# A conditioned hybrid decoder layer: adaLN sums of three row tiles on VectorE, adaLN columns through HBM, HGRN2's output gates by column

## The chip, the cores and the metric

The kernel runs on one core of a Trainium2 chip. A core has TensorE for matrix products, VectorE and ScalarE for elementwise work, GpSimd as a slower helper, and SyncE (SP), whose queue issues nearly all of this kernel's DMAs. The metric is device time in microseconds of one execution. The kernel before took 730.64 us, the median of 3 runs (730.37 to 730.97).

## The reference, cut to what matters

The layer works on x of 512 tokens by 1024 columns, with a conditioning vector c of 1024.

```python
cs = silu(c)
mod = cs @ w_ada + b_ada                      # 6 x 1024
sh1, sc1, gt1, sh2, sc2, gt2 = split(mod, 6)
h = rmsnorm(x, norm1_g) * (1 + sc1) + sh1
z = h @ w_in                                  # 3352 columns: hq hf hi hg | q kc vc ks vs kw vw g
o_hg  = hgrn2(hq, hf, hi, hg)                 # 4 heads of 128; rmsnorm(o, norm_g) * silu(hg) at its end
o_nsa = nsa(...)                              # 8 heads of 64, rope on q and k, three branches
x = x + gt1 * (concat(o_hg, o_nsa) @ w_out)
h2 = rmsnorm(x, norm2_g) * (1 + sc2) + sh2
a, v = split(causal_dwconv(h2 @ w_up, conv_w, conv_b), 2)
x = x + gt2 * ((silu(a) * v) @ w_down)
```

Rope turns the first 16 columns of each 64-wide head by angles that depend on the token's position and eight fixed frequencies.

## The kernel before, in words

All dense products are done with operands split into a high and a low part in a rounded 32-bit format, three matmuls for one product (`mm3`: high by high, high by low, low by high; lines 132, 133 and 134 of the profile). `split` makes the parts: ScalarE copies the high part (line 128), VectorE subtracts it for the low part (line 129). The order of all instructions is written out by hand: every engine works through its own list in the order of the program, and generators are interleaved by `emit`.

**First projection (lines 567 to 606).** The 1024 columns of h are eight row tiles k of 128 (columns of h lie on partitions, tokens run along the free dimension). For each k, four accumulators `accq` (one for each 128 tokens) and two `accf` take 18 matmuls of 512 columns. Ahead of use, h of tile k+1 is made: `ada_row(k+1)` sums cs times w_ada's two 128-wide columns for shift and scale with eight matmuls of 32 stationary columns (line 384, into the tile that the warm-up used before, so the rows read `warm<-ada,cs`), ScalarE copies the 256 sums (line 388), and `ada_col` turns them into two columns with two matmuls against a selecting vector `sel` (line 395). `h_tile` then makes the factors on VectorE (lines 399, 400), applies them on ScalarE (line 417), copies the high part on ScalarE (line 418) and subtracts on VectorE (line 419). The row matmuls stand in front of tile k's 18 matmuls, the column after the first three.

The loads of this stage come in order on SP's queue: x, then for each k four pieces of w_ada (line 280, 1 MB in all), a piece of the q weights (line 299) and, for every second k, one of the forget-gate weights (line 302). In the step k = 0, after the loads of tile 3, `load_small` loads the rest of the constants (263 KB; masks and rope frequencies), the positions and the gains (lines 313 to 317). The first weights of the k and v projection follow (line 206). The rope tables (`all_tables`) are made in five steps, one after each `h_tile`: nothing, gate tables, first reduction of the angle, second reduction, sine and cosine with GpSimd's products.

**Attention beside dense work (about 120 to 304 us).** The generator `attn` does scores, exponents, transpositions (`F`, line 991) and values (`oT`, line 1019) in units. ScalarE copies the transposed probabilities out (line 998) into tiles of a pool of 32 buffers that also holds most long-lived tiles. Beside it run HGRN2's level products and the dense projections. `proj_tok` gives tokens on partitions with 256-wide matmuls (tile `pt`); `proj_T` gives columns on partitions with 512-wide ones (tile `pT`, written `pT<-hT,whi`). HGRN2's gates (`hg_gate_out`) come from `proj_tok`. Each of the two takes eight steps per pair of heads. Every few units attention calls the next step of `adas`: for the second sub-layer's shift and scale, `ada_cols` multiplies a quarter (256 columns) of w_ada by cs (line 1241), ScalarE copies the sums, and two matmuls against a column of ones (line 1272) make columns of them, which VectorE adds to the bias. `ada_rows` does likewise for gt1, spread over all partitions.

**Output projection (304 to 372 us).** For each 128 tokens i, `hg_mix` multiplies HGRN2's values, normalises on VectorE (line 1206) and multiplies by the gates (line 1209); `hg_flip` transposes (line 1217) and makes the high part on ScalarE and the low part on VectorE (lines 1220, 1221) with the norm's gain. `out_mm` multiplies by w_out, first attention's half, then HGRN2's. From 345 us on the second norm uses `a2` and `sh2` (lines 1412, 1414), and the up and down projections follow to the end.

Of the kernel before, what the change touches and what calls it, by code (L numbers as in the profile page):

```python
# [19 lines left out]
P = 128  # L20
# [30 lines left out]
PREP4 = ('', 'la1 na3 fa3', '', 'la2', '', 'la3', '', '')  # L51
LEVELS = (1, 2, 4, 8, 16, 32, 64)

C_IDENT = 0
C_LMASK = 128
# [3 lines left out]
C_INV = C_BLK + 4  # L59
C_ANY = C_INV + 8  # L60
# [28 lines left out]
def hybrid_layer_kernel(ctx: ExitStack, tc: tile.TileContext, d: dict, out: bass.AP, dbg=None):  # L89
# [8 lines left out]
    psum = ctx.enter_context(tc.tile_pool(name="psum", bufs=8, space=PSUM))  # L98
    ctx.enter_context(tc.manual_schedule())
# [132 lines left out]
    def piece(g=False):  # L232

        name, _, _ = loads[taken[0] - 1] if ahead_raw else loads[taken[0]]
        if not ahead_raw:
            raw = take(name)
            if name.startswith(("hq", "hf", "hvo")):
# [25 lines left out]
    sc.dma_start(cb[:, 0:P], d["consts"][:, 0:P])  # L263
# [48 lines left out]
    def load_small():  # L312
        sp.dma_start(cb[:, P:], d["consts"][:, P:])
# [63 lines left out]
    def ada_row(k):  # L377

        c0 = k % 2 * 256
        for j in range(KT):
            g = 32 * (j % 4)
            pe.matmul(rows[g:g + 32, c0:c0 + 256], cs32[:, j],
                      ada[k][j // 4][:, j % 4].rearrange("p e c -> p (e c)"),
                      start=(j < 4), stop=(j >= 4), skip_group_check=True)
        t = TMP([P, 256], tag="row")
        sc.copy(t, rows[:, c0:c0 + 256])
        return t

    def ada_col(k, t):

        adc = adcs[0][:, 2 * k:2 * k + 2]
        for e in range(2):
            pe.matmul(adc[:, e:e + 1], t[:, e * P:e * P + P], sel, start=True, stop=True)
        return adc
# [36 lines left out]
    def gate_tables():  # L433
        gp.tensor_copy(identb, ident)
        gp.tensor_copy(causb, cb[:, C_CAUS:C_CAUS + P])
# [17 lines left out]
    def all_tables():  # L453
        yield
# [4 lines left out]
        sc.copy(ctab, gains.unsqueeze(1).to_broadcast([P, NT, 4, HD]))  # L459
# [16 lines left out]
        for m in (2048.0, 1.0):  # L476
# [4 lines left out]
            yield  # L481
        ve.tensor_scalar(ang, ang, 3.1415925, -3.1415925, ALU.min, ALU.max)
        sc.activation(sn, ang, AF.Sin)
        sc.activation(co, ang, AF.Sin, scale=0.5)
        ve.tensor_tensor(co, co, co, ALU.mult)
# [67 lines left out]
    row = ada_row(0)  # L553
# [3 lines left out]
    adc = ada_col(0, row)  # L557
# [10 lines left out]
    for k in range(KT):  # L568
        h = hT[k]
        if k + 1 < KT:  # L570
# [9 lines left out]
            wn = first_weights(k + 1)  # L580
            wfn = first_gates(k + 1)
        if k == KT - 1:
            for _ in tables:
                pass
            piece()
        if k == 0:
            for e, f in ((0, 0), (0, 1), (1, 0)):
# [3 lines left out]
                if e + f == 0:  # L591
                    row = ada_row(1)
                elif f:
                    h_tile(1, ada_col(1, row))
                    next(tables, None)
        for i in range(NT if k else 0):
            sl = slice(i * P, (i + 1) * P)
            if k + 1 < KT and i == 1:
                h_tile(k + 1, ada_col(k + 1, row))
                next(tables, None)  # L600
# [4 lines left out]
        if k + 1 < KT:  # L605
            w, wfk = wn, wfn
# [565 lines left out]
    def hg_gate_out(pr):  # L1172
        def f(hb, a):
            if hb == 0:
                HGT[pr] = G([NT, 256], s="hgt")
# [10 lines left out]
    def hg_mix(i):  # L1186
# [21 lines left out]
        for pr in range(2):  # L1208
            ve.tensor_tensor(on[:, 2 * pr:2 * pr + 2], on[:, 2 * pr:2 * pr + 2],
                             HGT[pr][:, i].rearrange("p (h e) -> p h e", h=2), ALU.mult)  # L1210
        ons[i] = on

    def hg_flip(i):
# [5 lines left out]
        pv = ps.rearrange("p (h t) -> p h t", h=4)  # L1219
        sc.activation(m[:, 0], pv, AF.Copy, scale=hgg)  # L1220
        ve.scalar_tensor_tensor(m[:, 1], pv, hgg, f32(m[:, 0]), ALU.mult, ALU.subtract)
# [41 lines left out]
    def ada_cols(s, dst, bias, gain=None):  # L1263

        for q in range(4):
            sums = ada_quarter()
            rows = TMP([P, 512], tag="arow")
            sc.activation(rows[:, 0:256], sums, AF.Copy, scale=1.0 / 32)
            yield
            ps = PS()  # L1270
            for k in range(2):
                pe.matmul(ps[:, k:k + 1], rows[:, k * P:(k + 1) * P], ones[:, 0:1], start=True, stop=True)
            sl = slice(2 * q, 2 * q + 2)
            ve.tensor_tensor(dst[:, sl], ps[:, 0:2], bias[:, sl], ALU.add)
            if gain is not None:
                ve.tensor_tensor(dst[:, sl], dst[:, sl], gain[:, sl], ALU.mult)
            yield
# [66 lines left out]

    kv = proj_kv()
# [102 lines left out]
    out_mm(0, 0, KN)  # L1448
    hg_mix(1)
# [144 lines left out]
```

## Time and profile before

| what | value |
|---|---|
| median of 3 runs | 730.64 us |
| the profiled execution's own time | 730.55 us |
| its span, first to last instruction | 728.8 us |
| TensorE busy | 722.0 us (99%) |
| VectorE, ScalarE, GpSimd busy | 423.5, 329.5, 107.2 us |
| DMA moved | 90.22 MB, 124 GB/s on average |
| granted TensorE clock, mean | 0.999 |

Times are microseconds from the span's start. PE is TensorE's matmul queue, PEld its weight loads, DVE is VectorE, ACT ScalarE, POOL GpSimd, SPq SyncE's queue of DMA issues. A matmul's duration reaches past the start of the next, since matmuls are pipelined: what one costs is the distance between starts.

### The profile page before, as it was taken

Reading aid. Unit: us, or ns where it says so; the run is one execution under the profiler, and the core shown is the slowest. Engines: PE = TensorE matmul, PEld = TensorE weight load, DVE = VectorE, ACT = ScalarE, POOL = GpSimd, SP = SyncE. Lnnn points to the kernel's source line nnn. Section 1 sums busy time; section 2 is a strip of 40 time slices with the busy share of each in tenths; the row PEclk is TensorE's granted clock in tenths of the full one; section 3 lists DMA queues with packets and bytes.
Section 4 is the critical chain, followed back from the end, with each engine's and each line's share of the span. In section 5 each row is a group of like instructions: output and inputs, shape, how many; then the busy total and the mean of one; then the engine's idle time right before and its main releaser. Section 6 shows DMA issues by size and latency. Waiting matters only on the chain.

```text
span 728.8 us, 10806 instructions
## 1 busy us (share of the span) xinstructions
PE 722.0 (99%) x4275; PEld 595.0 (82%) x4275; DVE 423.5 (58%) x804; ACT 329.5 (45%) x632; POOL 107.2 (15%) x99
## 2 busy tenths in 40 slices
PE   8999999999999999999999999999999999999997
PEld 4678898787888888888898888888888888888886
DVE  5447587856867775567856666665555455224223
ACT  5555446655557565634563354344343443121220
POOL 1013020200000000010006536541101101000000
PEclk9999999999999999999999999999999999999999
DMA  9984171365233311724223534533442431325311
GB/s 287 289 261 130 33 232 58 126 185 164 92 130 117 116 59 59 270 77 121 59 58 116 174 98 133 167 84 96 116 113 62 116 115 61 114 86 174 98 47 58
DMA packets 109319, 90.22 MB, mean 124 GB/s; under 512 B 5555, under 2 KB 95187, under 8 KB 109269
## 3 DMA queue, kind: packets, MB, share of 16 engines
q1 hardware_dynamic: 109013, 89.43, 40.3%
q8 instruction: 34, 0.56, 0.3%
q10 hardware_dynamic: 256, 0.10, 0.1%
q14 instruction: 16, 0.13, 0.1%
HBM read 87.42 MB, written 2.10 MB: 123 GB/s over the span
## 4 chain that ended last, share of the span: by engine, by line
PE 92%; SPq 3%; DMA 2%; DVE 1%; issue 0%; ACT 0%; ACTq 0%
PE u L132 11%; PE u L133 11%; PE u L134 11%; PE dn L133 5%; PE dn L134 5%; PE dn L132 5%; PE oT L1019 3%; PE F L991 3%; PE pT L132 2%; PE pT L134 2%; PE pT L133 2%; PE oh L132 2%; PE oh L134 2%; PE oh L133 2%; PE S L939 2%; SPq L280 2%
## 5 line engine op out<-in xcount | busy, mean ns | idle before, releaser
L129 DVE TENSOR_TENSOR wlo<-raw,whi 128x1024 fp32r<-128x1024 f32 (+1 forms) x87 | 111.8, 1285 | 146.3 <-ACT whi L128 145.9
L132 PE MATMUL u<-h2h,whi 128*128 128x512 f32 (+1 forms) x360 | 136.7, 380 | 0.0
L133 PE MATMUL u<-h2l,whi 128*128 128x512 f32 (+1 forms) x360 | 136.7, 380 | 0.0
L134 PE MATMUL u<-h2h,wlo 128*128 128x512 f32 (+1 forms) x360 | 136.7, 380 | 0.0
L128 ACT CAST whi<-raw 128x1024 fp32r<-128x1024 f32 (+1 forms) x87 | 89.8, 1032 | 96.1 <-PE dn L134 80.0
L134 PEld LDWEIGHTS u<-h2h,wlo 128*128 128x128 f32 x360 | 67.7, 188 | 12.9
L132 PEld LDWEIGHTS u<-h2h,whi 128*128 128x128 f32 x360 | 67.7, 188 | 12.8
L133 PEld LDWEIGHTS u<-h2l,whi 128*128 128x128 f32 x360 | 67.7, 188 | 12.7
L133 PE MATMUL dn<-wlo,gT 128*128 128x512 f32 x160 | 62.3, 390 | 0.0
L134 PE MATMUL dn<-whi,gT 128*128 128x512 f32 x160 | 62.3, 389 | 0.0
L132 PE MATMUL dn<-whi,gT 128*128 128x512 f32 x160 | 62.2, 389 | 0.0
L356 POOL TENSOR_TENSOR hrs<-hrs,mhalf 128x4 f32<-128x4 f32 (+2 forms) x16 | 17.7, 1112 | 238.2 <-DVE hrs L355 238.2
L1500 POOL TENSOR_TENSOR y<-y,y 128x512 f32<-128x512 f32 x22 | 28.4, 1290 | 165.1 <-DVE y L1495 161.4
L128 ACT CAST gT<-y 128x512 fp32r<-128x512 f32 x20 | 12.4, 622 | 71.1 <-POOL y L1500 71.1
L960 ACT ACTIVATE pt<-S,mx 128x128 f32<-128x128 f32 (+3 forms) x64 | 33.8, 533 | 17.6 <-DVE mx L943 17.4
L129 DVE TENSOR_TENSOR gT<-y,gT 128x512 fp32r<-128x512 f32 x20 | 15.6, 782 | 42.8 <-ACT gT L128 42.8
L998 ACT COPY pT<-F 128x512 f32<-128x512 f32 (+2 forms) x52 | 26.2, 504 | 24.5 <-PE F L991 24.5
L1498 ACT ACTIVATE y<-y 128x512 f32<-128x512 f32 x22 | 13.9, 632 | 50.4 <-DVE y L1495 50.4
L943 DVE TENSOR_REDUCE mx<-S 128x1 f32<-128x384 f32 (+3 forms) x48 | 28.4, 597 | 14.2 <-PE S L941 14.1
L133 PEld LDWEIGHTS dn<-wlo,gT 128*128 128x128 f32 x160 | 30.0, 188 | 6.5 <-DVE wlo L129 0.2
L132 PEld LDWEIGHTS dn<-whi,gT 128*128 128x128 f32 x160 | 30.0, 188 | 6.3
L134 PEld LDWEIGHTS dn<-whi,gT 128*128 128x128 f32 x160 | 30.0, 188 | 6.1
(335 smaller groups left out, 1511.1 us busy)
## 6 DMA issues: line engine op xcount, KB each, us to landing
raw<-in_w_up SPq DMA_DIRECT2D x44, 512.0 KB, 4.0
aw<-in_w_ada SPq DMA_DIRECT2D x12, 1024.0 KB, 5.3
raw<-in_w_down SPq DMA_DIRECT2D x10, 1024.0 KB, 5.2
ada<-in_w_ada SPq DMA_DIRECT2D x32, 256.0 KB, 5.9
raw<-in_w_in SPq DMA_DIRECT2D x7, 1024.0 KB, 6.6
x<-in_x SPq DMA_DIRECT2D x8, 512.0 KB, 5.5
raw<-in_w_cmp SPq DMA_DIRECT2D x8, 512.0 KB, 4.9
raw<-in_w_out SPq DMA_DIRECT2D x4, 1024.0 KB, 5.0
```

The costliest lines, as they stand in the source:

```text
L128: sc.copy(hi, src)
L129: (eng or ve).tensor_tensor(lo, src, f32(hi), ALU.subtract)
L132: pe.matmul(o, ah, bh, start=start, stop=False, skip_group_check=True)
L133: pe.matmul(o, ah, bl, start=False, stop=False, skip_group_check=True)
L134: pe.matmul(o, al, bh, start=False, stop=stop, skip_group_check=True)
L356: gp.tensor_tensor(o, o, mhalf[:, 0:n], ALU.pow)
L943: ve.tensor_reduce(mx[:, 0:n], ps[:, 0:n * W].rearrange("p (b w) -> p b w", b=n), AX.X, ALU.max, negate=True)
L960: sc.activation(pt[:, sl], ps[:, sl], AF.Exp, bias=mx[:, e:e + 1], accum_out=su[:, h % 2, e:e + 1])
L991: pe.transpose(ps[:, j * P:(j + 1) * P], src[:, j * P:(j + 1) * P], ident)
L998: sc.copy(pT, ps[:, 0:n * P])
L1019: pe.matmul(oTs[i][r:r + 64, h // 2], VV[:, j, b, g], src[:, q * P:(q + 1) * P], start=(h == 0 and b == 0 and j == 0), stop=False, skip_gr ...
L1500: gp.tensor_tensor(ys[0], ys[0], y, ALU.mult)
```

## The change

It has five parts.

- The adaLN rows of tiles 4, 6 and 7 are no longer summed on TensorE. `ada_sum` does it on VectorE: eight instructions of 128x256 that multiply w_ada's piece by cs per partition and add up; the column is then made against a vector of ones. The steps are placed inside `h_tile` of tiles 3, 5 and 6, one tile earlier than the column's use: four, five and five of them before the subtraction for the low part of h, the rest behind it. The place of the column among the matmuls changes for tiles 4, 6 and 7, and the last tile's high part comes directly from the scaling.
- The small loads go before the loads of tile 3, the 263 KB of masks behind those of tile 7, and the frequencies of rope come with the first load of constants. The steps of the rope tables are cut differently and are made after tiles 1, 2, 4, 5 and 7.
- `ada_cols` no longer makes columns on TensorE. The four partial rows of each vector are stored to HBM, read back as 64 rows of 128 after attention, transposed once and added up on VectorE (`cols_sum`).
- HGRN2's gates are projected by column (`proj_T`). They are multiplied in after the transposition in `hg_flip`, together with the gain, and the split follows.
- The piece of the k and v weights for the end of the first projection is made before the last tables.

```diff
+ROWS = (2, 3, 5)
+COLS = (0, 0, 1, 1, 2, 1, 2, 2)
+SUMS = {3: (4, 4, 4), 5: (6, 5, 3), 6: (7, 5, 3)}
+QUICK = 7
...
+    def ada_sum(k):
+        t = TMP([P, 2, P], tag="rows")
+        arow[k] = t, ones[:, 0:1]
+        for j in range(KT):
+            w = ada[k][j // 4][:, j % 4]
+            if j:
+                ve.scalar_tensor_tensor(t, w, cs[:, j:j + 1], t, ALU.mult, ALU.add)
+            else:
+                ve.tensor_scalar(t, w, cs[:, 0:1], None, ALU.mult)
+            yield
...
     def h_tile(k, adc):
...
-        sc.activation(xk, xk, AF.Identity, bias=sh1[:, k:k + 1], scale=a1[:, k:k + 1])
-        sc.copy(h[:, 0], xk)
+        if k == QUICK:
+            sc.activation(h[:, 0], xk, AF.Identity, bias=sh1[:, k:k + 1], scale=a1[:, k:k + 1])
+            t = TMP([P, T], tag="ht")
+            ve.tensor_scalar(t, xk, a1[:, k:k + 1], sh1[:, k:k + 1], ALU.mult, ALU.add)
+            xk = t
+        else:
+            sc.activation(xk, xk, AF.Identity, bias=sh1[:, k:k + 1], scale=a1[:, k:k + 1])
+            sc.copy(h[:, 0], xk)
+        if k in SUMS:
+            sums = ada_sum(SUMS[k][0])
+            for _ in range(SUMS[k][1]):
+                next(sums)
         ve.tensor_tensor(h[:, 1], xk, f32(h[:, 0]), ALU.subtract)
         hT.append(h)
+        if k in SUMS:
+            for _ in range(SUMS[k][2]):
+                next(sums)
...
+                if k == 0:
+                    load_small()
                 load_ada()
                 load_qf()
-                if k == 0:
-                    load_small()
+                if k == 4:
+                    sp.dma_start(cb[:, C_LMASK:], d["consts"][:, C_LMASK:])
...
-            if k:
-                row = ada_row(k + 1)
+            if n in ROWS:
+                ada_row(n)
...
-            if k + 1 < KT and i == 1:
-                h_tile(k + 1, ada_col(k + 1, row))
-                next(tables, None)
+            if n < KT and i == COLS[n]:
+                h_tile(n, ada_col(n))
+                if k in (1, 3, 4, 6):
+                    next(tables, None)
...
     def hg_gate_out(pr):
-            ve.scalar_tensor_tensor(HGT[pr][:, 2 * hb:2 * hb + 2].rearrange("p i c -> p (i c)"), th, 1.0, a,
-                                    ALU.add, ALU.mult)
+            ve.scalar_tensor_tensor(HGT[pr][:, j], th, 1.0, a, ALU.add, ALU.mult)
...
-        for pr in range(2):
-            ve.tensor_tensor(on[:, 2 * pr:2 * pr + 2], on[:, 2 * pr:2 * pr + 2],
-                             HGT[pr][:, i].rearrange("p (h e) -> p h e", h=2), ALU.mult)
...
-        sc.activation(m[:, 0], pv, AF.Copy, scale=hgg)
-        ve.scalar_tensor_tensor(m[:, 1], pv, hgg, f32(m[:, 0]), ALU.mult, ALU.subtract)
+        t = TMP([P, 4, P], tag="og")
+        for pr in range(2):
+            ve.scalar_tensor_tensor(t[:, 2 * pr:2 * pr + 2], ps[:, pr * 256:pr * 256 + 256]
+                                    .rearrange("p (h t) -> p h t", h=2), hgg,
+                                    HGT[pr][:, :, i * P:(i + 1) * P], ALU.mult, ALU.mult)
+        split(m[:, 0], m[:, 1], t)
...
     def ada_cols(s, dst, bias, gain=None):
+        rows = G([D], s="arow")
         for q in range(4):
             sums = ada_quarter()
-            rows = TMP([P, 512], tag="arow")
-            sc.activation(rows[:, 0:256], sums, AF.Copy, scale=1.0 / 32)
+            sc.copy(rows[:, q * 256:q * 256 + 256], sums)
             yield
-            ps = PS()
-            for k in range(2):
-                pe.matmul(ps[:, k:k + 1], rows[:, k * P:(k + 1) * P], ones[:, 0:1], start=True, stop=True)
-            sl = slice(2 * q, 2 * q + 2)
-            ve.tensor_tensor(dst[:, sl], ps[:, 0:2], bias[:, sl], ALU.add)
+            if q == 3:
+                sp.dma_start(adr[4 * len(late_cols):4 * len(late_cols) + 4], rows[0:P:32])
+                late_cols.append((dst, bias, gain))
+            yield
+    adr = hbm.tile([8, D], F32, name="adr")
+    def cols_load():
+        r = TMP([64, P], tag="acol")
+        sp.dma_start(r, adr.rearrange("g (k p) -> (g k) p", p=P))
+        return r
+    def cols_sum(r):
+        ps = PS()
+        pe.transpose(ps[:, 0:64], r, ident[0:64, 0:64])
+        for n, (dst, bias, gain) in enumerate(late_cols):
+            ve.tensor_reduce(dst, ps[:, 32 * n:32 * n + 32].rearrange("p (g k) -> p k g", g=4), AX.X, ALU.add)
+            ve.tensor_tensor(dst, dst, bias, ALU.add)
...
-    dense = chain(hv0, hg_value_odd(), proj_tok(hg_gate_out(0)), proj_tok(hg_gate_out(1), False), late())
+    dense = chain(hv0, hg_value_odd(), proj_T(hg_gate_out(0)), proj_T(hg_gate_out(1), False), late())
...
     for _ in adas:
         pass
+    acol = cols_load()
...
     out_mm(0, 0, KN)
+    cols_sum(acol)
     hg_mix(1)
```

## Rows read from the trace of the kernel before

**Rows 1.** The page: busy us, share of the span, instructions of each engine.
```profile
PE 722.0 (99%) x4275; PEld 595.0 (82%) x4275; DVE 423.5 (58%) x804; ACT 329.5 (45%) x632; POOL 107.2 (15%) x99
```
**Rows 2.** Stretches: length, then busy time of PE, PEld, DVE, ACT, POOL.
```profile
146.00:304.00 158.00, 158.00 (x1432) 132.27 (x1431) 103.24 (x255) 94.79 (x228) 0.00 (x0) 1.00 0.41 132
```
**Rows 3.** Stretches, row tiles k=6 and k=7 of the first projection.
```profile
52.15:57.88 5.73, 5.73 (x40) 4.36 (x40) 2.21 (x6) 3.28 (x5) 0.00 (x0) 1.00 0.32 90
57.88:61.95 4.07, 4.07 (x19) 3.38 (x18) 2.55 (x5) 2.96 (x4) 1.59 (x1) 1.00 0.97 323
```
**Rows 4.** The chain that ended last, 30 to 47 us: start, length, what.
```profile
33.09 7.79 DMA ada<-in_w_ada
```
**Rows 5.** Timeline of TensorE, first projection: start, duration, what.
```profile
34.41 1.07 PE L384 MATMUL warm<-ada,cs 128*32 128x256 f32 x16
35.41 0.50 PE L132 MATMUL accq<-wq,hT 128*128 128x512 f32 x1
...
36.22 0.50 PE L395 MATMUL adc<-sel,row 128*128 128x1 f32 x4
...
47.92 0.40 PE L134 MATMUL accq<-wq,hT 128*128 128x512 f32 x1
...
53.73 0.40 PE L134 MATMUL accq<-wq,hT 128*128 128x512 f32 x1
```
**Rows 6.** VectorE groups by shape: count, busy us, mean ns, idle before.
```profile
L862 DVE SCALAR_TENSOR_TENSOR chs<-cth,cps 128x256 f32<-128x256 f32 x1 | 0.4, 421 | 0.6 <-ACT cth L860 0.6
```
**Rows 7.** Timeline of VectorE, first projection.
```profile
43.31 0.21 DVE L400 SCALAR_TENSOR_TENSOR a<-adc,bsc,vt 128x1 f32<-128x1 f32 x1
...
51.79 0.69 DVE L419 TENSOR_TENSOR hT<-xnT,hT 128x512 fp32r<-128x512 f32 x1 [1.54 <-ACT hT L418]
```
**Rows 8.** Timeline of SP's DMA issues, w_ada's tiles 5, 6 and 7.
```profile
31.46 3.51 SPq L280 DMA_DIRECT2D ada<-in_w_ada  x4
...
36.37 3.79 SPq L280 DMA_DIRECT2D ada<-in_w_ada  x4
...
42.05 3.00 SPq L280 DMA_DIRECT2D ada<-in_w_ada  x4
```
**Rows 9.** Stretches of 2 us; the last number is GB/s moved.
```profile
26.00:28.00 2.00, 2.00 (x10) 1.66 (x9) 0.53 (x3) 1.40 (x3) 0.00 (x0) 1.00 1.05 305
28.00:30.00 2.00, 2.00 (x21) 0.98 (x21) 1.25 (x6) 0.90 (x6) 0.00 (x0) 1.00 0.76 188
...
48.00:50.00 2.00, 2.00 (x12) 1.69 (x11) 1.60 (x3) 0.89 (x2) 2.00 (x4) 1.00 1.07 365
```
**Rows 10.** Timeline of TensorE, one quarter's columns and what follows.
```profile
254.97 0.50 PE L1272 MATMUL ps<-ones,arow 128*128 128x1 f32 x4
255.41 1.53 PE L1019 MATMUL oT<-pT,VV 128*64 128x128 f32 x24
```
**Rows 11.** Stretch, line 1272 alone: length, PE busy, PEld busy.
```profile
146.00:304.00 158.00, 4.13 (x32) 4.28 (x32) 1.00 0.41 132
```
**Rows 12.** Timeline of SP's issues, end of attention.
```profile
292.71 2.11 SPq L1446 DMA_DIRECT2D x<-in_x  x4
```
**Rows 13.** Timeline of TensorE: one step of each projection and its successor.
```profile
208.36 0.48 PE L132 MATMUL pT<-hT,whi 128*128 128x512 f32 x1
...
209.82 0.49 PE L991 MATMUL F<-cb,pt 128*128 128x128 f32 x3
...
250.94 0.36 PE L132 MATMUL pt<-whi,hT 128*128 128x256 f32 x1
...
252.45 0.49 PE L991 MATMUL F<-cb,pt 128*128 128x128 f32 x3
```
**Rows 14.** Timelines of VectorE and TensorE, HGRN2's last mixed tile.
```profile
330.52 0.75 DVE L1221 SCALAR_TENSOR_TENSOR mixH<-ps,hgg,mixH 128x512 fp32r<-128x512 f32 x1 [2.24 <-ACT mixH L1220]
...
335.01 0.39 PE L132 MATMUL oh<-woh,mixH 128*128 128x512 f32 x1
```
**Rows 15.** Stretch, line 998 alone: length, ScalarE busy and copies.
```profile
142.00:254.00 112.00, 14.97 (x31) 1.00 0.46 142
```

More of the change, by code (lines that the diff above doesn't have):

```diff
@@ L51 @@
 PREP4 = ('', 'la1 na3 fa3', '', 'la2', '', 'la3', '', '')
+ROWS = (2, 3, 5)
+COLS = (0, 0, 1, 1, 2, 1, 2, 2)
+SUMS = {3: (4, 4, 4), 5: (6, 5, 3), 6: (7, 5, 3)}
+QUICK = 7
 LEVELS = (1, 2, 4, 8, 16, 32, 64)
 C_IDENT = 0
-C_LMASK = 128
+C_INV = 128
+C_LMASK = 136
 C_CMASK = C_LMASK + sum(P // n for n in LEVELS)
@@ L58 @@
 C_BLK = C_CAUS + P
-C_INV = C_BLK + 4
-C_ANY = C_INV + 8
+C_ANY = C_BLK + 4
 C_COLS = C_ANY + NT
@@ L98, in hybrid_layer_kernel @@
     psum = ctx.enter_context(tc.tile_pool(name="psum", bufs=8, space=PSUM))
+    hbm = ctx.enter_context(tc.tile_pool(name="hbm", bufs=1, space=bass.MemoryType.DRAM))
     ctx.enter_context(tc.manual_schedule())
@@ L262, in hybrid_layer_kernel @@
     cb = cst.tile([P, C_COLS], F32, name="cb")
-    sc.dma_start(cb[:, 0:P], d["consts"][:, 0:P])
+    sc.dma_start(cb[:, 0:C_LMASK], d["consts"][:, 0:C_LMASK])
     ident = cb[:, C_IDENT:C_IDENT + P]
@@ L386, in ada_row, with ada_col @@
                       start=(j < 4), stop=(j >= 4), skip_group_check=True)
[L387 to L391, printed above, removed]
+        t = TMP([P, 2, P], tag="row")
+        sc.copy(t.rearrange("p e c -> p (e c)"), rows[:, c0:c0 + 256])
+        arow[k] = t, sel
+    def ada_sum(k):
[8 more added lines that the diff above has]
+            yield
+    arow = {}
+    def ada_col(k):
         adc = adcs[0][:, 2 * k:2 * k + 2]
+        t, one = arow.pop(k)
         for e in range(2):
-            pe.matmul(adc[:, e:e + 1], t[:, e * P:e * P + P], sel, start=True, stop=True)
+            pe.matmul(adc[:, e:e + 1], t[:, e], one, start=True, stop=True)
         return adc
@@ L458, in all_tables @@
         gp.tensor_scalar(gains[:, 0], gains[:, 0], HD ** -0.5, None, ALU.mult)
-        sc.copy(ctab, gains.unsqueeze(1).to_broadcast([P, NT, 4, HD]))
         posf = cst.tile([P, NT], F32, name="posf")
@@ L480, in all_tables @@
                 ve.scalar_tensor_tensor(ang, rnd, -pc * m, ang, ALU.mult, ALU.add)
-            yield
+            if m > 1.0:
+                yield
         ve.tensor_scalar(ang, ang, 3.1415925, -3.1415925, ALU.min, ALU.max)
+        sc.copy(ctab, gains.unsqueeze(1).to_broadcast([P, NT, 4, HD]))
+        yield
         sc.activation(sn, ang, AF.Sin)
         sc.activation(co, ang, AF.Sin, scale=0.5)
+        yield
         ve.tensor_tensor(co, co, co, ALU.mult)
@@ L552, in hybrid_layer_kernel @@
     x_scale(3)
-    row = ada_row(0)
+    ada_row(0)
     xn_out(2, 0, ve.tensor_copy, fl[2, 0])
@@ L556, in hybrid_layer_kernel @@
     xn_out(3, 0, ve.tensor_copy, fl[3, 0], (0,))
-    adc = ada_col(0, row)
+    adc = ada_col(0)
     fl[3, 1] = xn_flip(3, 1)
@@ L569, in hybrid_layer_kernel @@
         h = hT[k]
-        if k + 1 < KT:
+        n = k + 1
+        if n < KT:
             if k + 3 < KT:
+                if k == 0:
+                    load_small()
                 load_ada()
                 load_qf()
-                if k == 0:
-                    load_small()
+                if k == 4:
+                    sp.dma_start(cb[:, C_LMASK:], d["consts"][:, C_LMASK:])
             elif k + 3 == KT:
                 issue()
-            if k:
-                row = ada_row(k + 1)
-            wn = first_weights(k + 1)
-            wfn = first_gates(k + 1)
+            if n in ROWS:
+                ada_row(n)
+            wn = first_weights(n)
+            wfn = first_gates(n)
         if k == KT - 1:
+            piece()
             for _ in tables:
                 pass
-            piece()
         if k == 0:
@@ L591, in hybrid_layer_kernel @@
                 if e + f == 0:
-                    row = ada_row(1)
+                    ada_row(1)
                 elif f:
-                    h_tile(1, ada_col(1, row))
-                    next(tables, None)
+                    h_tile(1, ada_col(1))
+                    next(tables)
         for i in range(NT if k else 0):
             sl = slice(i * P, (i + 1) * P)
-            if k + 1 < KT and i == 1:
-                h_tile(k + 1, ada_col(k + 1, row))
-                next(tables, None)
+            if n < KT and i == COLS[n]:
+                h_tile(n, ada_col(n))
+                if k in (1, 3, 4, 6):
+                    next(tables, None)
             mm3(accq[i], h[:, 0, sl], h[:, 1, sl], w[:, 0], w[:, 1], False, k == KT - 1)
@@ L604, in hybrid_layer_kernel @@
             mm3(accf[j], wfk[:, 0, k % 2, sl], wfk[:, 1, k % 2, sl], h[:, 0], h[:, 1], k == 0, k == KT - 1)
-        if k + 1 < KT:
+        if n < KT:
             w, wfk = wn, wfn
@@ L1172, in hg_gate_out, with f @@
     def hg_gate_out(pr):
-        def f(hb, a):
-            if hb == 0:
-                HGT[pr] = G([NT, 256], s="hgt")
+        def f(j, a):
+            if j == 0:
+                HGT[pr] = G([2, T], s="hgt")
             th = TMP([P, T])
             sc.activation(th, a, AF.Tanh, scale=0.5)
-            ve.scalar_tensor_tensor(HGT[pr][:, 2 * hb:2 * hb + 2].rearrange("p i c -> p (i c)"), th, 1.0, a,
-                                    ALU.add, ALU.mult)
+            ve.scalar_tensor_tensor(HGT[pr][:, j], th, 1.0, a, ALU.add, ALU.mult)
         return f
@@ L1343, in part @@
             yield
+    gp.tensor_copy(causb, cb[:, C_CAUS:C_CAUS + P])
     kv = proj_kv()
```

11 lines of the change are left out of this document (4 added, 7 removed).

## The prediction, on record before the changed kernel was seen

> **What bounds the kernel now.** I read the page first: TensorE is busy 99% of the span and its weight loads 82%, everything else under 60% [rows 1]. The reader is to see one full engine, so what the change is worth is first a count of TensorE time taken away. Then I split the span with the table of stretches. Between 146 and 304 us (attention beside the dense projections) TensorE is busy all 158 us, VectorE 103, ScalarE 95 [rows 2]: removed TensorE time should come out in full there. From 304 to the end the matmuls stand back to back and the change adds one transposition. The place where TensorE is not alone is the first projection, up to 62 us. One row tile k with the adaLN row of the next costs 5.73 us of TensorE, the last one without costs 4.07 [rows 3]: 1.66 us are the row and the column. But the chain of waits names a DMA there: the last quarter of w_ada's tile 5, issued at 33.09, lands 7.79 us later, at 40.88, and TensorE's row waited for it [rows 4]. So that stage is held by TensorE and by the stream of loads almost at once, and each part has to be worked out against both.
>
> **The sums on VectorE.** On TensorE a row runs from 34.41 to 35.41, 1.00 us, and the switch to 32 columns and back shows as about 0.2 more (the first accq matmul behind it is 0.50 long, the others 0.40); the column, 0.36 from 36.22 on plus 0.09 for its switch, stays [rows 5]. Three rows go: 3 x 1.2 = 3.6 us, and 0.3 more if tile 5 is no longer waited for. This 3.9 is the upper bound of the stage.
> What is added: each sum is eight VectorE instructions of 128x256. The nearest row of that shape is 0.421 us [rows 6]; in a chain on one tile I take the whole 0.42 each, 3.3 us a sum, and 9.9 for three. VectorE is idle for 3.5 of the 5.73 us of a tile [rows 3], but it works in order, and the sums stand ahead of the lower half of h (0.69 us, [rows 7]), for which the next tile's third matmul waits. Sum 6 puts five steps ahead of it, and the fifth reads the second half of w_ada's tile.
> The loads: the last quarter of tile 5 lands 5.9 us after its issue ended at 34.97; the same from the issues of tiles 6 and 7, ended at 40.16 and 45.05, gives 46.1 and 51.0 [rows 4, 8]. These two are estimates. Moving 263 KB of constants behind tile 7 takes 263/305 = 0.87 us out of the stream in front of tiles 4 to 7; I take them 0.8 earlier. The small loads (positions, gains) now stand in front of tile 3. What they cost the stream: between 28 and 30 us it moved 188 GB/s where the two microseconds before had 305 [rows 9], so 0.23 MB or 0.8 us were lost; I take 0.8, with 0.4 (their 130 KB alone) and 1.2 as ends.
> The Trainium skill, DMA: Bandwidth & Descriptors, Specifications, says that transfers under 512 bytes fall below line rate, and the positions are runs of 4 bytes; by bytes alone tile 3 would come in time, by this rule and the dip that agrees with it the row of tile 3 is about 0.3 us late, which the wait for tile 5 swallows again. The sum is the same by either.
> Step by step: tile 5 lands at 40.1, its row is done at 40.65, so k=4 starts its matmuls 0.95 earlier than now and ends at 45.3. VectorE has the factor of h for k=5 at 43.52 now [rows 7], then 0.8 earlier, at 42.75. Four steps of sum 6 (1.7 us) are done before its second half lands (46.1 - 0.8 = 45.3); the fifth ends at 45.7, the lower half of h at 46.4. The third matmul of k=5, now at 47.92 [rows 5], starts at 46.45: 1.5 gained, where 2 were there without the wait. Behind it on VectorE: three steps (to 47.65), two weight splits of 0.69 (49.0), the factors (49.35), five steps of sum 7 (51.4; its tile is there at 50.2), the lower half of h (52.1). The third matmul of k=6, now at 53.73 [rows 5], starts at 52.1. The column of tile 7 then waits 0.35 for the last three steps. k=7 starts at 56.6 instead of 57.88 [rows 3]. I take 1.3 us for the stage. If the loads land no earlier, the same chain gives 0.5; if 1.5 earlier, VectorE alone holds it and it gives 2.2; if nothing waits, 3.9. Below: a loss of 0.7, where a step costs 0.55 instead of 0.42.
> The last tile's h without the copy, the earlier piece of the kv weights, and the other places of the rope tables: their instructions run on ScalarE and GpSimd, which have 2.4 us and more free per tile [rows 3], and nothing of this stage reads the tables. Nothing; 0.3 late at most.
>
> **adaLN columns by HBM.** Per quarter, two matmuls against a column of ones go: four records from 254.97 to 255.41, 0.44 us [rows 10]; all 32 records keep TensorE busy 4.13 [rows 11]. Eight quarters: 3.5 (start to start) to 4.1; I take 3.8. Added: one transposition of 64 rows, 0.2 at most. Net 3.6, nearly all in the full stretch. The two stores sit on SP's queue behind w_ada loads and wait for a ScalarE copy that follows the row at once; the weight load behind them slips by that wait, some 0.4 us, and is issued a whole load ahead of its use: nothing, or 0.4 each. The read back is queued ahead of the x loads at 292.71 [rows 12], over 35 us after the last store can have gone, and its transposition stands behind row tile 0's first output matmuls, over 10 us later. Hidden; without that cover TensorE would wait the 6 us of a load [rows 4] once.
>
> **HGRN2's gates by column.** A step of twelve 256-wide matmuls takes 252.45 - 250.94 = 1.51 us, a step of six 512-wide ones 209.82 - 208.36 = 1.46 [rows 13]. Sixteen steps: 0.7 us (0 to 1.0). The two multiplications by the gate leave VectorE in front of the transpositions, and behind them two come from PSUM, then a copy and a subtraction: each mixed tile is about 0.7 us later. The last is ready at 331.3 now and is wanted at 335.01 [rows 14], so 3.7 us of cover hide it. The first transposition waits 0.1 less. Take 0.1.
>
> **Sum.** 1.3 + 3.6 + 0.7 + 0.1 = 5.7. The profiled execution took 730.55 us (span 728.8 and 1.75 around it), 0.09 under the median of the runs, so 730.55 - 5.7 = 724.85; I say 724.8.
>
> **Rivals.**
> A. Nothing in the first stage waits, and TensorE's rows go in full: 3.9 + 4.4 = 8.3, 722.2. For: the steps are divided before and behind the subtraction, and VectorE has 3.5 us free per tile against 3.3 for a sum. Against: the landing at 40.88 [rows 4] holds TensorE already, and 3.5 free is no surplus.
> B. The first stage gives nothing: loads arrive as now and VectorE's order takes back the rows. 730.55 - 4.4 = 726.1. For: the stream still moves 365 GB/s at 48 to 50 us [rows 9], so it is full to the end. Against: 0.87 us leave it.
> C. The attention stretch does not give the time back: with 4 us of 158 gone TensorE begins to wait for VectorE or ScalarE. 730.55 - 1.4 = 729.1. For: they feed it in turn at every step. Against: TensorE has no idle time in 158 us with VectorE at 65% [rows 2].
> D. Slower: the rows of two column sets now hold one of the 32 large buffers for four quarters each, from 142 to 254 us, and attention's transposed probabilities take theirs from the same pool. 31 copies of them fall in that time [rows 15], 15 pairs. If each pair must wait for oT matmuls that read an older one (24 of them take about 1.46 us, [rows 10]) and half of it reaches TensorE, that is 15 x 0.73 = 11: 730.55 - 5.7 + 11 = 735.9. It decides from 0.38 us a pair. Against: now these copies follow TensorE's transpositions and wait for no buffer.
>
> **How the numbers follow.** The forecast with its own range 723.0 to 727.0 has 0.57, A 0.20, B 0.12, C 0.05, D 0.06. The range has to hold A with the upper ends of the other terms (730.55 - 3.9 - 4.1 - 1.0 - 0.2 = 721.3) and B with their lower ones and the loss of 0.7 (730.55 - 3.3 + 0.7 = 728.0): 721.3 to 728.0. About 0.2%, 1.5 us, is what a measurement of this kernel can tell from no change; faster by more are the forecast, A and B, 0.89, within it C, 0.05, slower D, 0.06.
>
> **What would show it.** Right: three of the eight groups of row matmuls on ada gone; k=7's first matmul near 56.6; no matmul on arow; the gates' steps at 1.46; TensorE without idle time from 146 on, and the later marks earlier by 5 to 6 us. Wrong: steps of the sums clearly off 0.42; the lower half of h for k=5 not held by w_ada's tile 6; copies of the probabilities that wait for oT; a gap of TensorE at the transposition of the columns. The prediction fails if the first stage gives 3 us or more, or if the attention stretch shrinks by less than 3.

## The result, and the profile after

The changed kernel takes 726.15 us (median of 6 runs, 725.73 to 726.85) against 730.60 us of the kernel before (6 runs beside them, 730.37 to 730.97): ratio 0.994, 95% interval 0.9927 to 0.9953, so 4.45 us less. The forecast was 724.8 us, and 726.15 lies inside its range. The profiled execution took 726.3 us, its span is 724.5.

The page after, answering [rows 1]: TensorE is as full as before, with 176 matmuls and 6.5 us of busy time fewer; VectorE is 10.7 us busier.

```profile
PE 715.5 (99%) x4099; PEld 583.7 (81%) x4100; DVE 434.2 (60%) x822; ACT 327.4 (45%) x628; POOL 107.3 (15%) x99
```

Where the 4.3 us of the span come from is read from the first matmul of each stage in TensorE's timeline. Two of these marks before, and the first of them after:

```profile
61.95 0.39 PE L132 MATMUL kva<-whi,hT 128*128 128x512 f32 x1
304.78 1.06 PE L1197 MATMUL hgo<-hv,hgA 128*128 128x128 f32 x8
```

```profile
60.82 0.39 PE L137 MATMUL kva<-whi,hT 128*128 128x512 f32 x1
```

The key and value projection (kva), where the first projection ends, starts at 60.82 instead of 61.95: 1.13 us. From there to the first matmul of HGRN2's output (hgo, the end of attention) it is 239.00 us instead of 242.83: 3.83. The output projection, up to the transposition of the tile `crow`, takes 38.48 instead of 38.40. From there on 0.6 us are lost again. About half of it is one late weight tile in the up projection, which no other run here shows. The rest, 0.25, lies at the very end: the span runs 3.84 us on from the start of the last addition, where it was 3.59.

First the first projection. The stretch with the columns of tile 7, and the last tile, as in [rows 3], with the stretch of k=5 ahead of them; the columns are length, then busy time of TensorE, its weight loads, VectorE, ScalarE, GpSimd:

```profile
45.98:50.96 4.98, 4.84 (x24) 3.75 (x22) 4.77 (x13) 3.32 (x8) 0.00 (x0) 1.00 0.99 341
50.96:56.74 5.78, 5.14 (x24) 3.67 (x22) 5.24 (x13) 1.80 (x3) 0.26 (x1) 1.00 0.30 71
56.74:60.82 4.08, 4.08 (x20) 3.38 (x18) 2.39 (x5) 2.96 (x4) 4.08 (x7) 1.00 1.04 350
```

k=6 has no row of its successor any more, and still takes 5.78 us where it took 5.73: VectorE is busy for 5.24 of them, TensorE no longer all the time. TensorE's timeline (start, duration, what, and in brackets the idle time and who ended it), answering [rows 5]:

```profile
35.83 0.39 PE L139 MATMUL accq<-wq,hT 128*128 128x512 f32 x1
36.87 0.61 PE L414 MATMUL adc<-ones,rows 128*128 128x1 f32 x4 [0.65 <-DVE rows L402]
...
47.11 0.39 PE L139 MATMUL accq<-wq,hT 128*128 128x512 f32 x1
47.64 0.61 PE L414 MATMUL adc<-ones,rows 128*128 128x1 f32 x4
...
51.19 0.39 PE L138 MATMUL accq<-wq,hT 128*128 128x512 f32 x1
51.98 0.50 PE L139 MATMUL accq<-wq,hT 128*128 128x512 f32 x1 [0.41 <-DVE hT L448]
...
52.80 0.40 PE L139 MATMUL accq<-wq,hT 128*128 128x512 f32 x1
53.42 0.61 PE L414 MATMUL adc<-ones,rows 128*128 128x1 f32 x4 [0.22 <-DVE rows L402]
```

Matmuls in a row start 0.23 apart. The column of tile 4 starts 1.04 after the matmul ahead of it (0.81 lost), tile 6's 0.53 after (0.30), tile 7's 0.62 (0.39), and the third matmul of k=6 0.79 (0.56). Together 2.06 us, and after each late column the next matmul follows at 0.47 instead of 0.36, another 0.33: 2.4 of the 3.6 us that the three rows gave are waited away, each time for VectorE. VectorE's timeline says why (a line with xN is N steps, from the start of the first to the end of the last). First the start of tile 4's sum, then sum 6:

```profile
32.34 0.35 DVE L404 TENSOR_SCALAR rows<-ada,cs 128x256 f32<-128x256 f32 x1 [0.36 <-DMA ada<-in_w_ada]
...
43.00 0.21 DVE L419 SCALAR_TENSOR_TENSOR a<-adc,bsc,vt 128x1 f32<-128x1 f32 x1
43.12 0.34 DVE L404 TENSOR_SCALAR rows<-ada,cs 128x256 f32<-128x256 f32 x1
43.50 2.05 DVE L402 SCALAR_TENSOR_TENSOR rows<-ada,cs,rows 128x256 f32<-128x256 f32 x4
45.47 0.68 DVE L448 TENSOR_TENSOR hT<-xnT,hT 128x512 fp32r<-128x512 f32 x1
46.07 1.52 DVE L402 SCALAR_TENSOR_TENSOR rows<-ada,cs,rows 128x256 f32<-128x256 f32 x3
47.50 0.69 DVE L134 TENSOR_TENSOR wq<-raw,wq 128x512 fp32r<-128x512 f32 x1
```

Sum 4 begins 0.36 us late, for the load of its tile; so that part of the 0.81 lost at its column is the load stream's, and not the chain's. Run e3 below, with the same first projection, bears this out: its tile 3 came late, its sum 4 found the load there, and TensorE's marked wait at that column is 0.31 instead of 0.65. In sum 6 there is no idle time, and none of its steps waits for a load. Four steps take 2.05: with 0.485 for one, they start (2.05 - 0.485) / 3 = 0.52 apart. From 43.12 to 47.50, without the 0.60 of the h subtraction in its middle, sum 6 takes 3.78 us.

The attention stretch, answering [rows 2], up to its new end, and the marks in it: a gates' step (1.47 from its first matmul to F's), and the transposition of the columns between two matmuls of other work.

```profile
146.00:299.82 153.82, 153.82 (x1303) 122.58 (x1300) 102.40 (x243) 94.47 (x223) 0.00 (x0) 1.00 0.42 134
```

```profile
225.19 0.47 PE L137 MATMUL pT<-hT,whi 128*128 128x512 f32 x1
...
226.66 0.49 PE L1029 MATMUL F<-cb,pt 128*128 128x128 f32 x3
...
299.82 1.06 PE L1234 MATMUL hgo<-hv,hgA 128*128 128x128 f32 x8
...
303.22 0.39 PE L139 MATMUL oh<-woh,mixN 128*128 128x512 f32 x1
303.54 0.27 PE L1323 MATMUL ps<-cb,acol 64*128 64x64 f32 x1
303.75 0.49 PE L1234 MATMUL hgo<-hv,hgA 128*128 128x128 f32 x2
```

TensorE is still without a gap there, and VectorE at 67%. What ScalarE's copies of the transposed probabilities wait for (line 1036, the line of rival D) is only TensorE's own transpositions:

```profile
L1036 ACT COPY pT<-F x52: 361/506/606, 129.0 to 297.5; 128x512 f32<-128x512 f32 x24, 128x384 f32<-128x384 f32 x16, 128x256 f32<-128x256 f32 x12
...
  PE F L1029: 22.7, 22
```

### The profile page after: what moved, and what is told of

Read it like the earlier page. It is cut to its first block, busy times and chain, and to the rows that moved or that the text cites. A ratio compares the mean times of both kernels' runs of the same rounds, so it can differ in the third digit from the quotient of the medians.

```text
span 724.5 us, 10465 instructions
## 1 busy us (share of the span) xinstructions
PE 715.5 (99%) x4099; PEld 583.7 (81%) x4100; DVE 434.2 (60%) x822; ACT 327.4 (45%) x628; POOL 107.3 (15%) x99
## 4 chain that ended last, share of the span: by engine, by line
PE 91%; DVE 3%; DMA 2%; SPq 2%; issue 1%; ACT 0%; ACTq 0%; DVEq 0%
PE u L139 11%; PE u L137 11%; PE u L138 11%; PE dn L138 6%; PE dn L137 6%; PE dn L139 5%; PE pT L137 3%; PE pT L139 3%; PE pT L138 3%; PE F L1029 3%; PE oT L1057 3%; PE oh L137 2%; PE oh L139 2%; PE oh L138 2%; PE S L977 2%; PE lev L1133 2%
## 5 line engine op out<-in xcount | busy, mean ns | idle before, releaser
L138 PE MATMUL dn<-wlo,gT 128*128 128x512 f32 x160 | 62.3, 390 | 0.0
L139 PE MATMUL dn<-whi,gT 128*128 128x512 f32 x160 | 62.3, 389 | 0.0
L137 PE MATMUL pT<-hT,whi 128*128 128x512 f32 x96 | 41.3, 430 | 0.0
L139 PE MATMUL pT<-hT,wlo 128*128 128x512 f32 x96 | 37.8, 394 | 0.0
L138 PE MATMUL pT<-hT,whi 128*128 128x512 f32 x96 | 37.5, 391 | 0.0
```

Source lines behind the costliest of these rows:

```text
L137: pe.matmul(o, ah, bh, start=start, stop=False, skip_group_check=True)
L138: pe.matmul(o, ah, bl, start=False, stop=False, skip_group_check=True)
L139: pe.matmul(o, al, bh, start=False, stop=stop, skip_group_check=True)
```

## The experiments

The theory: the change takes TensorE time away in three places, and the attention gives it back in full, but in the first projection VectorE, whose chained steps start 0.52 us apart, takes back 2.4 of 3.6 us (some 0.36 of it for the load of tile 4). The rivals: the load stream holds that stage; the gains lie elsewhere than in the removed instructions; 0.52 us is what the shape costs.

Eight kernels were timed in five rounds each, four at a time beside the kernel before (730.83 and 730.54 us). "Stage" is the time from the column of row tile 3 to the first kva matmul, the part of the first projection in which the sums lie, in the one profiled execution of each kernel. It leaves out what the loads of tiles 1 to 3 cost: the column of tile 3 stands anywhere from 30.41 to 31.82 us. The changed kernel, e2 and e3 have the same first projection, and their stages lie between 29.66 and 30.14, so a difference of half a microsecond in this column proves nothing by itself. Of e6 and e8 four executions are on record, of the changed kernel six.

| kernel | median us | ratio to before (95%) | stage us |
|---|---|---|---|
| before | 730.60 | 1 | 31.54 |
| changed | 726.15 | 0.9940 (0.9927 to 0.9953) | 29.98 |
| e1_rows_back | 727.51 | 0.9955 (0.9942 to 0.9967) | 31.20 |
| e2_ones_back | 728.46 | 0.9964 (0.9952 to 0.9977) | 30.14 |
| e3_gates_back | 726.88 | 0.9943 (0.9931 to 0.9956) | 29.66 |
| e4_two_sums | 724.85 | 0.9920 (0.9906 to 0.9933) | 28.70 |
| e5_late | 725.29 | 0.9925 (0.9912 to 0.9937) | 28.64 |
| e6_two_late | 723.80 | 0.9906 (0.9893 to 0.9920) | 27.85 |
| e7_four_sums | 726.41 | 0.9943 (0.9931 to 0.9956) | 30.05 |
| e8_loads_back | 724.06 | 0.9908 (0.9893 to 0.9924) | 28.22 |

**The rows back on TensorE.**

```diff
-ROWS = (2, 3, 5)
-COLS = (0, 0, 1, 1, 2, 1, 2, 2)
-SUMS = {3: (4, 4, 4), 5: (6, 5, 3), 6: (7, 5, 3)}
+ROWS = (2, 3, 4, 5, 6, 7)
+COLS = (0, 0, 1, 1, 1, 1, 1, 1)
+SUMS = {}
```

> All six later row tiles' adaLN sums are again eight TensorE matmuls each (no VectorE sums, columns in their old place); the columns by way of HBM, the gates by column, the loads' order and the tables' steps stay. Theory (the stage gains what TensorE loses less what it waits for VectorE's chained steps): the first projection ends at about 61.9 us of the span in place of 60.8, and the run takes about 727.3 us against 726.15 of the changed kernel. Rival 1 (the load stream holds the first stage, the 1.1 us came from the loads' and tables' new order): still 60.8, 726.2 us. Rival 2 (the order of loads and tables itself costs something that the sums make up for): beyond 62.3, 727.8 us or more.

Measured: 727.51 us and a stage of 31.20 us, 1.22 more than with the sums. As the theory has it: three rows are worth 1.2 us of the 3.6 that they take. Beside the kernel before (31.54) the stage is 0.34 shorter without any sum, and no TensorE instruction waits for tile 5 now: before, its row was cut in two, at 40.22 and 41.01, and the next matmul followed 1.36 after its start; now it follows after 1.00. That is the wait that [rows 4] showed, gone with the new order of the loads (which part of that order did it was not tried). But the rows of tiles 2 and 3 were late in this run, and its first kva matmul stands at 62.33. By that mark rival 2 (beyond 62.3) would hold, by the time, 727.51 against 727.8 or more, it does not.

**The columns by ones again.**

```diff
-        rows = G([D], s="arow")
...
-            sc.copy(rows[:, q * 256:q * 256 + 256], sums)
+            rows = TMP([P, 512], tag="arow")
+            sc.activation(rows[:, 0:256], sums, AF.Copy, scale=1.0 / 32)
             yield
-            if q == 3:
-                sp.dma_start(adr[4 * len(late_cols):4 * len(late_cols) + 4], rows[0:P:32])
+            ps = PS()
+            for k in range(2):
+                pe.matmul(ps[:, k:k + 1], rows[:, k * P:(k + 1) * P], ones[:, 0:1], start=True, stop=True)
...
-    acol = cols_load()
...
-    cols_sum(acol)
```

> The eight quarters of the two adaLN columns are again summed by two 128x1 matmuls each against ones in the attention; no way by HBM, no transposition after it; all else as changed. Theory (16 matmuls of 0.22 us leave TensorE's in-order queue and nothing comes back): attention longer by 3.6 us, out projection shorter by 0.2: about 729.6 us. Rival (part of the attention's 3.84 us came from the other instructions' places, since the share that the planner gives out changes): 727.5 to 728.5 us. That the change did nothing there: 726.2.

Measured: 728.46 us. In its trace the 32 records are back, four of them 0.43 from the next instruction:

```profile
253.61 0.50 PE L1309 MATMUL ps<-ones,arow 128*128 128x1 f32 x4
254.04 1.20 PE L1057 MATMUL oT<-pT,VV 128*64 128x128 f32 x18
```

From kva to hgo it takes 242.36 us, 3.36 more than as changed; from hgo to the next stage's transpositions 38.08, 0.40 less. So the way by HBM is worth 2.96 us in the trace; the ratios put it at 0.9964 - 0.9940 = 0.0024, or 1.8 us, with intervals of 0.0013 on either side of each, and the medians differ by 2.3. By the time alone the rival (727.5 to 728.5) would do; but this run and the next give back 3.36 and 0.72 of the attention's 3.83 us, so nothing is left that came from elsewhere. The mechanism is the theory's; the size is below the 3.6, because a quarter cost 3.36 / 8 = 0.42, a little under the low end of 0.44, and the transposition with what it does to its neighbours 0.4 instead of 0.2. One cost more shows at the end: from the start of the last addition the span runs 3.55 us here and 3.59 before, but 3.83 to 3.92 in all eight kernels with the way by HBM. Why is not shown; it takes 0.3 of the 2.96.

**The gates by token again.**

```diff
-    dense = chain(hv0, hg_value_odd(), proj_T(hg_gate_out(0)), proj_T(hg_gate_out(1), False), late())
+    dense = chain(hv0, hg_value_odd(), proj_tok(hg_gate_out(0)), proj_tok(hg_gate_out(1), False), late())
...
+        for pr in range(2):
+            ve.tensor_tensor(on[:, 2 * pr:2 * pr + 2], on[:, 2 * pr:2 * pr + 2],
+                             HGT[pr][:, i].rearrange("p (h e) -> p h e", h=2), ALU.mult)
         ons[i] = on
```

> HGRN2's gates are again projected by token (128x256 tiles of the output, 16 steps) and multiplied in ahead of the transposition; all else as changed. Theory (a step of 12 matmuls of 512 columns takes 0.035 us less than one of 24 matmuls of 256 columns, 16 steps): 0.56 us longer, about 726.7 us. Rival (start-to-start sums within a shared queue only move charges between tiles): within 0.2 us of 726.15. Second rival (the multiplication on VectorE ahead of the transposition was on the path of the out projection): 727.5 us or more.

Measured: 726.88 us, 0.73 above the changed kernel's median; the intervals overlap, so by times alone it is open. The trace has from kva (60.70) to hgo (300.42) 239.72 us, 0.72 more than as changed, and 38.48 behind it, the same. Seven kernels here have the same attention, and their traces take 239.00 to 239.56 for it, so the 0.72 stands only just clear of that spread. The second rival (the multiplication in the way of the output projection) is out, and the theory's 0.56 is near. (A step is six matmuls of 512 columns or twelve of 256 [rows 13], half of what the expectation says.)

**Two accumulators.** Even parts in one, odd parts in another, joined by an addition: one VectorE instruction more a sum.

```diff
         t = TMP([P, 2, P], tag="rows")
+        u = TMP([P, 2, P], tag="rowo")
...
-            if j:
-                ve.scalar_tensor_tensor(t, w, cs[:, j:j + 1], t, ALU.mult, ALU.add)
+            s = u if j % 2 else t
+            if j > 1:
+                ve.scalar_tensor_tensor(s, w, cs[:, j:j + 1], s, ALU.mult, ALU.add)
             else:
-                ve.tensor_scalar(t, w, cs[:, 0:1], None, ALU.mult)
+                ve.tensor_scalar(s, w, cs[:, j:j + 1], None, ALU.mult)
+            if j == KT - 1:
+                ve.tensor_tensor(t, t, u, ALU.add)
```

> The three VectorE sums go into two accumulators, even and odd parts in turn, and one addition joins them, so that no step reads what the step ahead of it wrote. Theory A (the 485 ns of a step, 510 from start to start, come from its shape: two inputs of 128x256 in SBUF and one output): steps stay at 480 to 490 ns, a sum takes about 4.0 us again (two steps of 350, six of 485, one addition), and the time stays within 0.3 us of 726.15. Theory B (they come from reading the result of the step just before): steps of about 420 ns with 450 from start to start, a sum about 3.6 us or less, and the first projection ends some 0.3 to 0.8 us earlier, about 725.6 us.

Measured: 724.85 us, 1.3 below the changed kernel, a stage 1.28 shorter. VectorE's timeline of sum 6:

```profile
42.72 0.34 DVE L406 TENSOR_SCALAR rows<-ada,cs 128x256 f32<-128x256 f32 x1
42.98 0.35 DVE L406 TENSOR_SCALAR rowo<-ada,cs 128x256 f32<-128x256 f32 x1
43.24 0.48 DVE L404 SCALAR_TENSOR_TENSOR rows<-ada,cs,rows 128x256 f32<-128x256 f32 x1
43.64 0.48 DVE L404 SCALAR_TENSOR_TENSOR rowo<-ada,cs,rowo 128x256 f32<-128x256 f32 x1
44.04 0.48 DVE L404 SCALAR_TENSOR_TENSOR rows<-ada,cs,rows 128x256 f32<-128x256 f32 x1
44.44 0.68 DVE L452 TENSOR_TENSOR hT<-xnT,hT 128x512 fp32r<-128x512 f32 x1
...
45.83 0.48 DVE L404 SCALAR_TENSOR_TENSOR rowo<-ada,cs,rowo 128x256 f32<-128x256 f32 x1
46.34 0.43 DVE L408 TENSOR_TENSOR rows<-rows,rowo 128x256 f32<-128x256 f32 x1
46.68 0.69 DVE L134 TENSOR_TENSOR wq<-raw,wq 128x512 fp32r<-128x512 f32 x1
```

One step still shows 0.48 us, as theory A had it; but the steps start 0.40 apart instead of 0.52, a step starting before the one ahead of it has ended, so theory B is right where it matters, though it had put the gain (0.3 to 0.8 us) and the overlap too low. The addition itself, which reads both, starts 0.51 after the last step. Sum 6 takes 46.68 - 42.72 - 0.60 = 3.36 us instead of 3.78, with 9 instructions instead of 8. The Trainium skill, VectorE: DVE Perf Modes, Rules for kernel authors, advises to make chained VectorE instructions few, as the emptying of the pipe comes with each; here nine took 3.36 us and eight 3.78, so for these steps the measurement decides against that rule. The Trainium skill, VectorE: DVE Perf Modes, The DRAIN you can't avoid, adds that a next instruction that is not held starts earlier, which agrees with the 0.40 us between starts at 0.48 us each.

**The columns later**, with the sums as changed.

```diff
-COLS = (0, 0, 1, 1, 2, 1, 2, 2)
+COLS = (0, 0, 1, 1, 3, 1, 3, 3)
```

> The changed kernel with the columns of row tiles 4, 6 and 7 after three row tiles of the query product in place of two; the sums in one accumulator each, as changed. Theory (TensorE stands at the columns' matmuls for sums that VectorE has not finished: 0.8, 0.3 and 0.4 us): some 0.46 us of matmuls more lie ahead of each column, and the three waits shrink by 1.0 us together: about 725.2 us. Rival (VectorE's whole queue is what the stage runs by; a later column only makes the h tile late, and the wait moves to the next tile's first or third matmul): within 0.3 us of 726.2 us, with a wait of TensorE on hT in place of that on rows.

Measured: 725.29 us, 0.86 below the changed kernel, and a stage 1.34 shorter. The waits at the columns are gone; one at the h tile has grown from 0.41 to 0.71, as the rival had it:

```profile
37.76 0.50 PE L414 MATMUL adc<-ones,rows 128*128 128x1 f32 x4
...
48.12 0.50 PE L414 MATMUL adc<-ones,rows 128*128 128x1 f32 x4
...
52.12 0.50 PE L139 MATMUL accq<-wq,hT 128*128 128x512 f32 x1 [0.71 <-DVE hT L448]
53.84 0.50 PE L414 MATMUL adc<-ones,rows 128*128 128x1 f32 x4
```

So the place of the column was a good part of the matter: near the theory's size, with the rival's wait in one place of four. Of the two numbers 0.86 is the better one: this trace lost 1.12 us to the load of tile 3, ahead of the stage, and so found the load of tile 4 there, which saves the stage up to 0.36.

**Both together.** The two diffs above and nothing else.

> Two accumulators a sum and the later columns together. Two accumulators alone gave 724.85 us, with TensorE waiting 0.18 and 0.46 us at the columns of tiles 4 and 7. Theory: these two waits go and nothing comes in their place: 724.2 us. Rival (the wait moves to the h tile, as the column is 0.69 us later): 724.7 to 725.0 us.

Measured: 723.80 us, 0.4 below what the theory gave, and the lowest of all (e8 cannot be told from it); its interval lies wholly below the changed kernel's. The column of tile 7 and the end of the stage:

```profile
51.54 0.39 PE L139 MATMUL accq<-wq,hT 128*128 128x512 f32 x1
51.77 0.53 PE L418 MATMUL adc<-ones,rows 128*128 128x1 f32 x4
...
58.41 0.39 PE L137 MATMUL kva<-whi,hT 128*128 128x512 f32 x1
```

The column starts 0.23 after the matmul ahead of it, in TensorE's own rhythm. The stage is 31.20 - 27.85 = 3.35 us shorter than with all rows on TensorE, against 1.22 as changed: of the 3.6 that the prediction counted for three rows, nearly all. So what the changed kernel waited away was due to the chaining and the place of the columns. (Sum 4 waits 0.31 for its load here too, but with the later column TensorE does not wait for it.)

**A fourth sum**, that of tile 5, on VectorE too. Two things change with it: the column of tile 5 comes after three row tiles of the query product in place of one, and one step of sums 6 and 7 moves behind the h subtraction.

```diff
-ROWS = (2, 3, 5)
-COLS = (0, 0, 1, 1, 3, 1, 3, 3)
-SUMS = {3: (4, 4, 4), 5: (6, 5, 3), 6: (7, 5, 3)}
+ROWS = (2, 3)
+COLS = (0, 0, 1, 1, 3, 3, 3, 3)
+SUMS = {3: (4, 4, 4), 4: (5, 4, 4), 5: (6, 4, 4), 6: (7, 4, 4)}
```

> As two accumulators with later columns, and row tile 5's sum on VectorE too, in four of the six tiles then. Another row of TensorE goes, 1.2 us. Theory (in the first projection VectorE is the next bound: it idles some 2 us in steps k=3 and 4, and a sum costs it 3.5): TensorE gives back most of the 1.2 us in waits on VectorE: 724.0 to 725.2 us, no better than three sums by more than 0.3 us. Rival (each row taken off TensorE counts nearly in full where the columns are late enough): 1.0 us better than three sums, about 723.2 us.

Measured: 726.41 us, 2.6 slower than three sums; in this arrangement the rival is out, and the theory too mild. A row of 1.2 us is gone from TensorE and the stage is 2.2 longer. Stretches from 36 to 43 and from 43 to 48 us, with three sums (e6) and then with four:

```profile
36.00:43.00 7.00, 7.00 (x47) 5.20 (x47) 5.26 (x20) 4.09 (x7) 0.00 (x0) 1.00 1.14 312
43.00:48.00 5.00, 5.00 (x25) 4.19 (x24) 4.85 (x14) 3.57 (x7) 0.00 (x0) 1.00 1.13 314
```

```profile
36.00:43.00 7.00, 6.85 (x33) 5.01 (x32) 6.54 (x22) 2.91 (x4) 0.00 (x0) 1.00 1.14 314
43.00:48.00 5.00, 4.06 (x16) 2.39 (x14) 4.75 (x14) 4.08 (x7) 0.00 (x0) 1.00 1.11 315
```

VectorE goes from 5.26 of 7 us to 6.54, and TensorE now stands for the h tile, whose factors come from VectorE behind the sum:

```profile
45.38 0.50 PE L137 MATMUL accq<-wq,hT 128*128 128x512 f32 x1 [0.94 <-ACT hT L447]
```

The column of tile 5 stands at 41.67, its h is there 3.7 us later, where e6 took 2.7 (40.91 to 43.61): VectorE had the rope tables' steps and a weight split behind the sum, up to 43.55, before it came to the factors. So work put on an engine that was "idle 2 us" delayed all that stood behind it in its queue. But the column's later place has its share: only 2.6 us of matmuls, up to 44.29, were left behind it to cover this. What a fourth sum costs with the column of tile 5 where it was is not shown.

**The small loads back behind tile 3**, on top of the fastest.

```diff
-                if k == 0:
-                    load_small()
                 load_ada()
                 load_qf()
+                if k == 0:
+                    load_small()
```

> As two accumulators with later columns, with the small loads back behind the load of row tile 3 and of the weights beside it, as in the kernel before. Theory (the load stream holds only the rows of tiles 2 and 3, by 0.3 to 0.8 us together, because the small loads are ahead of tile 3): 0.3 to 0.5 us faster than with the loads as changed. Rival A (a load that arrives earlier is used no earlier, the column of its tile is late enough): no difference within 0.2 us. Rival B (the rope tables on VectorE now wait for the positions and stop the sum of tile 4): 0.3 us slower or more.

Measured: 724.06 us, 0.26 above e6, between rival A's 0.2 and rival B's 0.3, with intervals that overlap: no difference that can be told. The theory's gain did not come: the rows of tiles 2 and 3 stood at 22.99 and 28.81 and took 1.07 each in this trace and in that of e6 (22.93, 28.74). So the order of the small loads is not what holds the stage. The load stream is close, though: in this trace the fifth part of sum 6 waits 0.25 for w_ada, which it does in neither e6 nor the changed kernel.

## Why the prediction was right, and where its working was not

**The first stage, 1.3 forecast, 1.13 measured.** Nearly the right number, by the wrong working. The step that failed is the VectorE step: "in a chain on one tile I take the whole 0.42 each". It was 0.52: the 0.42 is the duration of a lone instruction with other operands [rows 6], this one takes 0.485, and in a dependent chain the next starts 0.035 after its end. A sum took 3.8 instead of 3.3. Nor did the load of tile 6 hold the lower half of h for k=5: VectorE began sum 6 at 43.12, and all eight steps ran without waiting for a load. The loads came earlier than the 0.8 us that were taken: the issue of tile 6 ended at 38.26 instead of 40.16, 1.9 earlier. By the prediction's own chain loads 1.5 earlier would have given 2.2 us; loads put too late and steps put too short cancelled, which is luck. The third matmul of k=5 did start at 46.43 (46.45 forecast), but since TensorE had come late itself, having lost 0.81 us at the column of tile 4; sum 4, with its wait of 0.36 for the load of tile 4, had not been worked out at all. The forecasts for k=6's third matmul (52.1; 51.98) and k=7 (56.6; 56.74) agree in the same way: a load wait that did not come, against slower steps that were not foreseen. The late row of tile 3 that the small loads were to cost cannot be seen: e6 and e8, with them ahead of tile 3 and behind it, have that row at 28.74 and 28.81. And the rope tables' steps, which the prediction gives to ScalarE and GpSimd, are in part VectorE's (1.5 us from 40.36 as changed); nothing waited for them there, but in e7 they stood ahead of the factors. e1 and e6 bracket it: 1.2 us as changed, 3.35 when almost nothing waits; the 3.9 put down as the upper bound contained 0.3 for the wait for tile 5, and e1 shows that 0.34 apart.

**The columns by HBM, 3.6 forecast, 2.96 in the traces.** The removed matmuls were worth 3.36 instead of 3.8, the transposition cost 0.4 instead of 0.2. The 0.3 us more at the end of the program is a cost that the prediction did not have; it comes off the 2.96. The trip itself was hidden, as argued: the matmul at 303.54 follows in turn.

**The gates, 0.7 forecast, 0.72 in the traces** (e3), one step 1.47 where 1.46 was said. The last mixed tile's later end was covered as argued: its split ends at 327.1 instead of 331.3, 0.7 later than the 4.9 us by which all else had moved, and TensorE comes to it without a gap. The 0.1 for the first transposition cannot be seen.

**The rivals.** A (nothing waits) did not come, yet e6 shows that it was nearly to be had: 723.8 where A said 722.2, with 3.35 instead of 3.9 in that stage and 0.6 less for the columns. B (nothing in the first stage) was off by 1.1 in the trace, and yet the total, 726.15, is B's number (726.1) rather than the forecast's: of the 1.4 us by which the gain fell short of the forecast, 0.2 lie in the first stage, 0.6 in the columns and 0.6 behind the output projection. C and D did not come: TensorE has no gap from 146 to 299.82, and the copies of the probabilities wait for no buffer.

## What to carry to other kernels

A chain of instructions that each read the result of the one before has its own price: read the distance between starts of such a chain, not the duration of a lone instruction, and split an accumulation in two where it stands in the way. Work moved to an engine with idle time is paid by what is queued behind it, so ask of each instruction behind it who waits, and put the consumer on the full engine as late as its own successor allows. A forecast that meets the number is no proof of its working; check it at each mark.

## What the runs showed of the hardware

VectorE's scalar_tensor_tensor of 128x256 in SBUF shows 0.48 us whether or not it reads what the one before wrote (changed kernel and e4), but the starts lie 0.52 us apart in the first case and 0.40 in the second: two of them overlap by 0.08. A tensor_scalar of the same size follows another after 0.26. TensorE waited 1.12 us for the load of row tile 3 in the trace of e5 and not at all in those of e6 and e7, which have the same loads in the same order. And the span ends 3.83 to 3.92 us after the start of the last addition in eight kernels that take the columns by HBM, 3.55 and 3.59 in the two that do not.
